# A third quadrant block in each first FFN, and the small parameter operations on GpSimd

## The chip, the cores and the metric

The kernel runs on one core of a Trainium2 chip. TensorE (PE) multiplies, VectorE (DVE) does elementwise work, ScalarE (ACT) copies and applies functions, GpSimd (POOL) does a few small operations and issues the accumulating DMAs, and SyncE's queue (SP) issues the loads. Weights and x lie in HBM; SBUF holds tiles of 128 partitions; matmuls write PSUM banks of 128x512 fp32. The metric is the device time of one execution in microseconds.

## What is computed

Two layers of a streaming encoder on x of 256 x 1024, fp32. Cut to what matters:

```python
x += 0.5 * postnorm(swiglu(prenorm(x)))      # first FFN, D_FF = 2816
x += postnorm(mixer(prenorm(x)))             # S5 scan beside chunk attention
x += 0.5 * postnorm(swiglu(prenorm(x)))      # second FFN

def swiglu(h, w_gate, w_up, w_down):
    return (silu(h @ w_gate) * (h @ w_up)) @ w_down

# S5's parameters, of the layer's inputs alone
dt = exp(log_dt); mag = exp(lr * dt); ang = li * dt
ab_re, ab_im = mag * cos(ang), mag * sin(ang)
den = lr * lr + li * li
f_re = ((ab_re - 1) * lr + ab_im * li) / den
f_im = (ab_im * lr - (ab_re - 1) * li) / den
```

## The kernel before, in words

The 256 rows are two row tiles t of 128. All weights come as 2 x 184 chunks of 128x1024 fp32, in the order of use: 66 of the first FFN, 52 of the mixer, 66 of the second FFN. `load` (line 461) has SP load a chunk into one of 12 `raw` buffers. `halves` (line 467) splits it: ACT copies it to `wh` (rounded, line 371), DVE computes `wl = raw - wh` (line 378), and each product is then three matmuls (line 418): x's high part by `wh` and `wl`, and x's low part by `wh`. For the chunks of `ADDED` (44, 47 and so on to 65 of a first FFN) ACT writes `-wh` into `wl`, and an accumulating DMA on POOL's queue (`add_to`, line 382) adds the chunk.

An FFN has six blocks of columns, five of 512 and one of 256. `ffn` (line 741) does a block in one of two ways. The plain way takes gate and up products for each t. The other, `seven` (line 649), cuts rows, the inner dimension and gate/up into quadrants and takes 7 products of sums of quadrants where the plain way has 8; each product is 12 matmuls of 128x512. The sums of the inputs are made once (`sums`). The weight sums are totals of two chunks each: `total` 1 and 2 on DVE, and totals 3 and 4 (`BY_DMA`) by ACT, which negates a chunk in place, and an accumulating DMA that adds another chunk to it. A quadrant block converts 18 chunks on DVE (14 of products, 4 of the down projection), and evacuates PSUM with DVE and ACT. The down products of a block run inside the block that follows. `SEVEN` (line 31) says which blocks go this way: before, 1 and 3 of each first FFN, and 1 to 4 of each second.

`prep` (line 797) computes S5's parameters for a layer: two exponentials by polynomials on 128x16 values (`exp`), sines and cosines on 128x112 values, the factors `fr` and `fi`, and tables `E` that DVE builds from `ecs` and `esn`. In the kernel before, all its elementwise operations but the memsets are on DVE. POOL's other work is the power of -0.5 of each norm (line 393).

The order is not that of the code. `Graph` records every operation with its engine, an estimated cost and a due time; `schedule` (line 209) places the operations one by one in a list schedule and so fixes the order on each engine; each engine then runs its list in that order. `PREP_AT` and `BIAS_AT` name the chunk whose mark the operations of `prep` and the loads of the attention bias have to follow. A mark of a chunk of a quadrant block stands at that block's start.

Of the kernel before, what the change touches and what calls it, by code (L numbers as in the profile page):

```python
# [17 lines left out]
ALU = mybir.AluOpType  # L18
AX = mybir.AxisListType

P = 128
# [6 lines left out]
SP_LR, SP_LI, SP_DT, SP_D, SP_B = 0, 16, 32, 48, 52  # L28

N_BLK = (512, 512, 512, 512, 512, 256)  # L30
SEVEN = (((1, 3), (1, 2, 3, 4)), ((1, 3), (1, 2, 3, 4)))
FFN_CHUNKS = 66
MIX_CHUNKS = 52
LAYER_CHUNKS = 2 * FFN_CHUNKS + MIX_CHUNKS
# [5 lines left out]
LAG = 3  # L40
TAU = 1.395
MARGIN = {"pre": 10.0, "edge": 4.0, "conv": 7.558, "conv0": 3.423, "task": 7.748, "att0": 37.576, "s50": 37.749, "att1": 28.585, "sums": 3.0, "s51": 29.753, "prep": 40.0}
PREP_AT = (3, 149)
BIAS_AT = 50
LOOK = 0.027
CAP = 5.417
WARM = 16
# [18 lines left out]
class View:  # L66
# [50 lines left out]
    def ap(self):  # L117
        t = self.buf.tile
        for s in self.steps:
            t = s(t)  # L120
        return t
# [202 lines left out]
class Kern:  # L324
# [51 lines left out]
    def tt(self, out, a, b, op):  # L376
        return self.g.op("dve", 0.07 + a.free_size() / 960, [out], [a, b],
                         lambda: self.nc.vector.tensor_tensor(out=out.ap(), in0=a.ap(), in1=b.ap(), op=op))  # L378
# [16 lines left out]
    def stt(self, out, a, s, b, op0=ALU.mult, op1=ALU.add):  # L395
        cost = 0.07 + a.free_size() / 960 + 0.061 * isinstance(s, View)
        return self.g.op("dve", cost, [out], [a, s, b], lambda: self.nc.vector.scalar_tensor_tensor(  # L397
            out=out.ap(), in0=a.ap(), scalar=ap(s), in1=b.ap(), op0=op0, op1=op1))

    def ts(self, out, a, s1, s2=None, op0=ALU.mult, op1=ALU.add):  # L400
        def fn():
            if s2 is None:
                self.nc.vector.tensor_scalar(out=out.ap(), in0=a.ap(), scalar1=ap(s1), scalar2=None, op0=op0)
            else:
                self.nc.vector.tensor_scalar(out=out.ap(), in0=a.ap(), scalar1=ap(s1), scalar2=s2, op0=op0, op1=op1)  # L405
        cost = 0.07 + a.free_size() / 1920 + 0.061 * isinstance(s1, View)
        return self.g.op("dve", cost, [out], [a, s1], fn)
# [333 lines left out]
    def ffn(self, l, f, normed):  # L741
# [5 lines left out]
        for b, wd in enumerate(N_BLK):  # L747
            if b in SEVEN[l][f]:
                if s is None:
# [47 lines left out]
    def prep(self, l):  # L797
        self.mode("prep", "bulk")
        if l == 0:
            self.S = [self.own(f"st{i}", [P, PAIRS, 65], F32) for i in range(2)]  # L800
        after = [self.g.ops[self.mark[(0, PREP_AT[l])]]]
        self.constants(after)
# [5 lines left out]
        self.bias = [[self.blk() for _ in range(2)] for _ in range(2)]  # L808
        early = [self.g.ops[self.mark[(0, l * LAYER_CHUNKS + BIAS_AT)]]]
        for par in range(2):  # L810
            for u in range(2):
                b = self.bias[par][u].rearrange("p (h k) -> p h k", k=256)
# [1 line left out]
                self.memset("pool", b[0:64, :, 192:256], MASK)  # L814
        self.prm = prm
        lr, li = prm[:, SP_LR:SP_LR + 16], prm[:, SP_LI:SP_LI + 16]
        ts, tt, stt = self.ts, self.tt, self.stt

        def tmp(nmx):
            return self.own(f"pt_{nmx}", [P, 16], F32)  # L820

        def exp(o, xin):
            n, r, p = tmp("en"), tmp("er"), tmp("ep")
            ib = self.own("pt_ei", [P, 16], I32)
            ts(n, xin, math.log2(math.e), MAGIC)
            ts(n, n, MAGIC, op0=ALU.subtract)
            stt(r, n, -0.693359375, xin)
            stt(r, n, 2.12194440054690583e-4, r)
            ts(p, r, 1.0 / 5040)
            for k in (720, 120, 24, 6, 2, 1):  # L830
                stt(p, p, 1.0 / k, r, ALU.add, ALU.mult)
            ts(n, n, -127.0, 128.0, ALU.max, ALU.min)
            ts(n, n, 127.0, 8388608.0, ALU.add, ALU.mult)
            self.copy(ib, n)
            stt(o, p, 1.0, ib.bitcast(F32), ALU.add, ALU.mult)

        dt, ld, mag, mag2 = tmp("dt"), tmp("ld"), tmp("mag"), tmp("mag2")
        exp(dt, prm[:, SP_DT:SP_DT + 16])
        tt(ld, lr, dt, ALU.mult)
        exp(mag, ld)  # L840
        tt(mag2, mag, mag, ALU.mult)
        self.mag2 = mag2
        self.act(self.mt[:, :, 1:], mag2.spread(63), AF.Copy)

        wk = [self.blk() for _ in range(2)]
        ang, k, z, sn, cs, m, a = (wk[i // 4][:, (i % 4) * 112:(i % 4) * 112 + 112] for i in range(7))
        angv = ang.rearrange("p (e j) -> p e j", j=16)
        tt(angv[:, 0, :], li, dt, ALU.mult)
        for e in range(1, 7):
            ts(angv[:, e, :], angv[:, 0, :], float(2 ** e))  # L850
        ts(k, ang, 2.0 / math.pi, MAGIC)
# [4 lines left out]
        stt(ang, k, -c1, ang)  # L856
        stt(ang, k, -c2, ang)
        stt(ang, k, -c3, ang)
        tt(z, ang, ang, ALU.mult)
        ts(sn, z, 1.0 / 362880)  # L860
        for q in (-1.0 / 5040, 1.0 / 120, -1.0 / 6):
            stt(sn, sn, q, z, ALU.add, ALU.mult)
# [8 lines left out]
        stt(a, m, -1.0, m, ALU.mult, ALU.max)  # L871
        ts(k, a, -1.0, 1.0)
        ts(a, a, -1.0, 2.0)
        tt(m, m, a, ALU.mult)
        ecs = self.own("ecs", [P, 7, 16], F32)
        esn = self.own("esn", [P, 7, 16], F32)
        ef, sf = ecs.rearrange("p e j -> p (e j)"), esn.rearrange("p e j -> p (e j)")
        tt(ef, cs, k, ALU.mult)
        tt(a, sn, m, ALU.mult)
        tt(ef, ef, a, ALU.subtract)  # L880
        tt(sf, sn, k, ALU.mult)
        tt(a, cs, m, ALU.mult)
        tt(sf, sf, a, ALU.add)
        self.ecs, self.esn = ecs, esn

        ar, ni, nr, den, fr, fi, q = (tmp(s) for s in ("ar", "ni", "nr", "den", "fr", "fi", "q"))
        tt(ar, mag, ecs[:, 0, :], ALU.mult)
        ts(nr, ar, 1.0, op0=ALU.subtract)
        tt(ni, mag, esn[:, 0, :], ALU.mult)
        tt(den, lr, lr, ALU.mult)  # L890
        tt(q, li, li, ALU.mult)
        tt(den, den, q, ALU.add)
        self.recip(den, den)
        tt(fr, nr, lr, ALU.mult)
        tt(q, ni, li, ALU.mult)
        tt(fr, fr, q, ALU.add)
        tt(fr, fr, den, ALU.mult)
        tt(fi, ni, lr, ALU.mult)
        tt(q, nr, li, ALU.mult)
        tt(fi, fi, q, ALU.subtract)  # L900
        tt(fi, fi, den, ALU.mult)

        def half(t, i):
            return t[:, 256 * i:256 * i + 256].rearrange("p (j h) -> p j h", h=16)
# [51 lines left out]
        for e in range(6):  # L956
            k = 2 ** e
# [286 lines left out]
def _one_k(w):  # L1244
    return w.reshape(-1, P, 1024)


def _ffn_chunks(g, u, d, seven):
    gu, dn = [], []
    o = 0  # L1250
    for wd in N_BLK:
        s = slice(o, o + wd)
        if wd == 512:
            gu.append(np.concatenate([_two_k(g[:, s]), _two_k(u[:, s])]))
        else:
            gu.append(_two_k(np.concatenate([g[:, s], u[:, s]], axis=1)))
        dn.append(_one_k(d[s]))
        o += wd
    out = [gu[0]]
    for i in range(1, len(N_BLK)):  # L1260
        if i in seven:
            out += [gu[i][:2], dn[i - 1][:1], gu[i][2:], dn[i - 1][1:]]
        else:
            out += [gu[i], dn[i - 1]]
    out.append(dn[-1])
    return np.concatenate(out)


def _pack(a):
    f = np.float32  # L1270
    wall = []
    for l in range(DEPTH):
        w_in = a["w_in"][l]
        wall.append(_ffn_chunks(a["ffn_w_gate"][l, 0], a["ffn_w_up"][l, 0], a["ffn_w_down"][l, 0], SEVEN[l][0]))
        for blk in (0, 2, 1, 3, 6, 7, 4, 5):
# [51 lines left out]
```

## Time and profile before

| | |
|---|---|
| median of 3 runs (lowest, highest) | 1128.24 us (1126.39, 1130.42) |
| the profiled execution | 1127.01 us |
| its span, first to last instruction | 1125.2 us |
| PE, DVE, ACT, POOL busy | 98%, 85%, 67%, 9% of the span |
| mean granted clock of PE | 0.997 |

Times in the rows count from the start of the span; the 1.8 us between span and execution lie around it. The first FFN of layer 0 takes about the first 190 us, with its block 1 up to about 60, and that of layer 1 begins about 570. An instruction's time in a row is longer than the distance to the next one's start where an engine overlaps the end of one with the start of the next: a DVE operation of 128x1024 shows 1.22 us, and the next starts 1.13 to 1.14 after it.

### The profile page before, as it was taken

How to read it: one execution, taken by the hardware profiler on the slowest of the kernel's cores; microseconds unless marked ns; L12 is line 12 of the kernel's file. 1: busy time of each engine (PE TensorE's matmuls, PEld its weight loads, DVE VectorE, ACT ScalarE, POOL GpSimd, SP SyncE). 2: the span in 40 equal slices, each digit the busy share in tenths (PEclk: the TensorE clock that was granted, in tenths of full speed). 3: DMA queues.
4: the chain of work that ended last, by engine and by line, in shares of the span. 5: the costliest groups of instructions: out<-in, count | busy, mean ns of one | idle time of the engine just before them, and what ended most of it. 6: DMA issues, size and time to landing. Idle time of an engine off the chain costs nothing.

```text
span 1125.2 us, 15956 instructions
## 1 busy us (share of the span) xinstructions
PE 1107.9 (98%) x5728; PEld 885.6 (79%) x5728; DVE 954.2 (85%) x1402; ACT 749.1 (67%) x1066; POOL 99.4 (9%) x131
## 2 busy tenths in 40 slices
PE   8999999999999999999999999999999999999997
PEld 6778788777788888788887888887777888888886
DVE  6998995895977899899899689778959679999983
ACT  6957686647754697577577476856486546878752
POOL 1101111000000031010030011100000002111100
PEclk9999999999999999999999999999999999999999
DMA  9885997545275557899658669964535664789941
GB/s 343 228 314 129 328 295 235 169 136 164 97 251 197 179 122 217 269 283 278 243 162 263 229 181 325 276 213 148 170 112 181 195 212 143 214 219 268 293 167 38
DMA packets 69487, 238.61 MB, mean 212 GB/s; under 512 B 8096, under 2 KB 8864, under 8 KB 69408
## 3 DMA queue, kind: packets, MB, share of 16 engines
q1 hardware_dynamic: 60192, 204.03, 51.2%
q0 software_dynamic: 9216, 33.56, 16.3%
q8 instruction: 45, 0.74, 0.3%
q14 instruction: 34, 0.28, 0.1%
HBM read 202.96 MB, written 1.05 MB: 181 GB/s over the span
## 4 chain that ended last, share of the span: by engine, by line
PE 87%; DVE 5%; issue 2%; ACT 2%; DMA 2%; POOL 1%; SPq 0%; POOLq 0%; DVEq 0%; ACTq 0%
PE ps L418 81%; PE ps L432 4%; DVE wl L378 3%; DMA raw<-in_wall_dram 2%; PE ps L424 1%; DVE blk L378 1%; ACT blk L371 1%; POOL s L393 1%; ACT wh L371 1%; DVE blk L397 1%; DVE raw L378 0%; SPq L354 0%; DVE x L397 0%; DVE s L405 0%; POOLq L1322 0%
## 5 line engine op out<-in xcount | busy, mean ns | idle before, releaser
L418 PE MATMUL ps<-wh,blk 128*128 128x512 f32 x2848 | 878.0, 400 | 4.5 <-DVE blk L378 2.3
L418 PEld LDWEIGHTS ps<-wh,blk 128*128 128x128 f32 x2848 | 530.4, 188 | 127.6 <-DVE blk L378 3.9
L371 ACT ACTIVATE wh<-raw 128x1024 fp32r<-128x1024 f32 (+1 forms) x442 | 456.9, 1053 | 261.0 <-PE ps L418 200.4
L378 DVE TENSOR_TENSOR wl<-raw,wh 128x1024 fp32r<-128x1024 f32 (+1 forms) x426 | 505.7, 1215 | 104.3 <-ACT wh L371 103.7
L418 PE MATMUL ps<-wl,blk 128*128 128x512 f32 x1424 | 524.4, 399 | 0.9 <-DVE wl L378 0.8
L418 PEld LDWEIGHTS ps<-wl,blk 128*128 128x128 f32 x1424 | 267.5, 188 | 63.4 <-DVE wl L378 2.5
L371 ACT ACTIVATE blk<-ps 128x512 fp32r<-128x512 f32 (+4 forms) x156 | 86.5, 561 | 54.8 <-PE ps L432 30.2
L378 DVE TENSOR_TENSOR blk<-ps,blk 128x512 fp32r<-128x512 f32 (+2 forms) x164 | 109.4, 672 | 13.1 <-ACT blk L371 12.7
L432 PE MATMUL ps<-ident,blk 128*128 128x128 f32 x432 | 74.7, 273 | 0.0
L382 POOL DMA_DIRECT2D raw<-raw x48 | 41.6, 867 | 341.3 <-ACT raw L371 261.8
L393 POOL TENSOR_TENSOR s<-s,mhalf 128x1 f32<-128x1 f32 x24 | 32.1, 1338 | 448.3 <-DVE s L405 448.2
L371 ACT ACTIVATE blk<-blk 32x128 f32<-32x128 f32 (+4 forms) x148 | 59.1, 400 | 12.4 <-DVE blk L378 8.6
L432 PEld LDWEIGHTS ps<-ident,blk 128*128 128x128 f32 x432 | 54.6, 140 | 15.9 <-PE ps L418 1.3
L371 ACT ACTIVATE blk<-ps,s 128x512 f32<-128x512 f32 (+1 forms) x68 | 43.7, 655 | 24.6 <-PE ps L418 20.4
L378 DVE TENSOR_TENSOR raw<-raw,raw 128x1024 f32<-128x1024 f32 x48 | 58.1, 1219 | 0.1
L371 ACT ACTIVATE raw<-raw 128x1024 f32<-128x1024 f32 x48 | 50.2, 1053 | 4.3 <-DVE raw L378 3.9
L378 DVE TENSOR_TENSOR blk<-blk,blk 128x512 f32<-128x512 f32 (+3 forms) x70 | 42.3, 627 | 0.0
L371 ACT ACTIVATE blk<-blk,s 128x128 f32<-128x128 f32 (+2 forms) x76 | 34.6, 486 | 6.7 <-DVE blk L378 6.6
L397 DVE SCALAR_TENSOR_TENSOR blk<-blk,s,blk 128x512 f32<-128x512 f32 x44 | 32.0, 746 | 0.9 <-ACT blk L371 0.8
L397 DVE SCALAR_TENSOR_TENSOR blk<-ps,s,blk 128x512 f32<-128x512 f32 (+1 forms) x24 | 15.8, 658 | 9.7 <-ACT blk L371 9.4
L382 POOL DMA_DIRECT2D wl<-raw x16 | 13.8, 865 | 111.7 <-ACT wl L371 56.3
L378 DVE TENSOR_TENSOR blk<-ps,raw 128x512 f32<-128x512 f32 x32 | 19.8, 681 | 4.2 <-PE ps L418 4.2
(100 smaller groups left out, 434.0 us busy)
## 6 DMA issues: line engine op xcount, KB each, us to landing
raw<-in_wall_dram SPq DMA_DIRECT2D x366, 512.0 KB, 5.3
raw<-raw POOLq DMA_DIRECT2D x48, 512.0 KB, 5.3
wl<-raw POOLq DMA_DIRECT2D x16, 512.0 KB, 7.2
gain<-in_gains_dram SPq DMA_DIRECT2D x22, 256.0 KB, 4.3
blk<-in_bias_dram SPq DMA_DIRECT2D x8, 256.0 KB, 4.8
raw<-in_wall_dram SPq DMA_DIRECT2D x4, 256.0 KB, 4.3
blk<-in_sp_dram SPq DMA_DIRECT2D x4, 256.0 KB, 9.3
x<-in_x_dram SPq DMA_DIRECT2D x3, 256.0 KB, 5.8
```

The source lines that it names most:

```text
L371: self.nc.scalar.activation(out=out.ap(), in_=in_.ap(), func=func, **k)
L378: lambda: self.nc.vector.tensor_tensor(out=out.ap(), in0=a.ap(), in1=b.ap(), op=op))
L382: lambda: self.nc.gpsimd.dma_start(out=out.ap(), in_=in_.ap(), accum_op=ALU.add), func="dma")
L393: lambda: self.nc.gpsimd.tensor_tensor(out=out.ap(), in0=a.ap(), in1=b.ap(), op=ALU.pow))
L397: return self.g.op("dve", cost, [out], [a, s, b], lambda: self.nc.vector.scalar_tensor_tensor(out=out.ap(), in0=a.ap(), scalar=ap(s), in1= ...
L418: return self.g.op("pe", cost, [out], [lhsT, rhs], lambda: self.nc.tensor.matmul(out.ap(), lhsT=lhsT.ap(), rhs=rhs.ap(), start=start, stop ...
L424: self.nc.tensor.matmul(out.ap(), lhsT=lhsT.ap(), rhs=rhs.ap(), start=start, stop=stop)
L432: lambda o=o, s=s: self.nc.tensor.transpose(o.ap(), s.ap(), self.ident.ap()))
```

## The change

Block 2 of each first FFN goes the quadrant way too, so blocks 1, 2 and 3 do in a row. In `prep` the helpers `ptt`, `ts` and `stt` put its elementwise operations up to `fr` and `fi` on POOL, at an estimated cost of 0.25 us plus 2.2 ns for an element of a partition; what has a maximum stays on DVE, and so do the casts, the reciprocal, `cmul` and the tables. An `stt` becomes two POOL operations with a tile `pt_mid` between. `prep` may begin at chunk 26 in place of 3 (layer 1: 206 in place of 149), which is the start of block 2; the bias loads follow chunk 62 in place of 50.

```diff
-SEVEN = (((1, 3), (1, 2, 3, 4)), ((1, 3), (1, 2, 3, 4)))
+SEVEN = (((1, 2, 3), (1, 2, 3, 4)), ((1, 2, 3), (1, 2, 3, 4)))
...
-PREP_AT = (3, 149)
-BIAS_AT = 50
+PREP_AT = (26, 206)
+BIAS_AT = 62
...
-        ts, tt, stt = self.ts, self.tt, self.stt
+        tt = self.tt
+        gp = self.nc.gpsimd
+
+        def put(out, ins, fn):
+            self.g.op("pool", 0.25 + out.free_size() * 0.0022, [out], ins, fn)
+
+        def ptt(out, a, b, op):
+            put(out, [a, b], lambda: gp.tensor_tensor(out=out.ap(), in0=a.ap(), in1=b.ap(), op=op))
+
+        def ts(out, a, s1, s2=None, op0=ALU.mult, op1=ALU.add):
+            if op0 == ALU.max:
+                self.ts(out, a, s1, s2, op0, op1)
+            elif s2 is None:
+                put(out, [a], lambda: gp.tensor_scalar(out=out.ap(), in0=a.ap(), scalar1=s1, scalar2=None, op0=op0))
+            else:
+                put(out, [a], lambda: gp.tensor_scalar(out=out.ap(), in0=a.ap(), scalar1=s1, scalar2=s2, op0=op0, op1=op1))
+
+        def stt(out, a, s, b, op0=ALU.mult, op1=ALU.add):
+            if op1 == ALU.max:
+                return self.stt(out, a, s, b, op0, op1)
+            n = out.free_size()
+            mid = self.own(f"pt_mid{n}", [P, n])
+            ts(mid, a, s, op0=op0)
+            ptt(out, mid, b, op1)
...
-        tt(ld, lr, dt, ALU.mult)
+        ptt(ld, lr, dt, ALU.mult)
...
-        tt(ef, cs, k, ALU.mult)
+        ptt(ef, cs, k, ALU.mult)
```

The remaining lines turn `tt` into `ptt` in the same way. What this does to the order on the engines (the numbers in names only tell buffers apart):

POOL in layer 0, before: after the last power of the first norm come the four accumulations of block 1 (totals 3 and 4), then those of block 3.

```order
L393 TENSOR_TENSOR s_69_312<-s_68_308,mhalf_74 128x1
L382 DMA raw_339<-raw_373 128x1024
L382 DMA raw_354<-raw_387 128x1024
L382 DMA raw_304<-raw_254 128x1024
L382 DMA raw_322<-raw_271 128x1024
L382 DMA raw_819<-raw_883 128x1024
L382 DMA raw_857<-raw_906 128x1024
L382 DMA raw_776<-raw_726 128x1024
```

POOL in layer 0, now: `pt_en`, `pt_den`, `pt_q`, `pt_mid` and `pt_er` are tiles of `prep`, `prm` its inputs.

```order
L382 DMA raw_333<-raw_367 128x1024
L382 DMA raw_348<-raw_381 128x1024
L382 DMA raw_298<-raw_248 128x1024
L832 TENSOR_SCALAR pt_en_486<-prm_459 128x16
L824 TENSOR_TENSOR pt_den_493<-prm_459 128x16
L830 TENSOR_SCALAR pt_en_486<-pt_en_486 128x16
L824 TENSOR_TENSOR pt_q_499<-prm_459 128x16
L830 TENSOR_SCALAR pt_mid_443_504<-pt_en_486 128x16
L382 DMA raw_316<-raw_265 128x1024
L824 TENSOR_TENSOR pt_er_518<-pt_mid_443_504,prm_459 128x16
L824 TENSOR_TENSOR pt_den_493<-pt_den_493,pt_q_499 128x16
```

Five operations of `prep` stand between the third and the fourth accumulation of block 1; 18 more and three memsets follow before the accumulations of block 2.

POOL in layer 1, before: the last power of the norm, the four accumulations of block 1, then block 3's first.

```order
L393 TENSOR_TENSOR s_1235_5645<-s_1234_5640,mhalf_74 128x1
L382 DMA raw_5505<-raw_5564 128x1024
L382 DMA raw_5529<-raw_5582 128x1024
L382 DMA raw_5443<-raw_5352 128x1024
L382 DMA raw_5486<-raw_5377 128x1024
L382 DMA raw_6103<-raw_6147 128x1024
```

POOL in layer 1, now, from the first accumulation of block 1 on; the rows left out are nine more operations of `prep`.

```order
L382 DMA raw_5444<-raw_5525 128x1024
L382 DMA raw_5482<-raw_5544 128x1024
L832 TENSOR_SCALAR pt_en_5774<-prm_5746 128x16
...
L830 TENSOR_SCALAR pt_mid_1691_5819<-pt_ep_5813 128x16
L824 TENSOR_TENSOR pt_ep_5813<-pt_mid_1691_5819,pt_er_5797 128x16
L830 TENSOR_SCALAR pt_mid_1692_5830<-pt_ep_5813 128x16
L824 TENSOR_TENSOR pt_ep_5813<-pt_mid_1692_5830,pt_er_5797 128x16
L382 DMA raw_5398<-raw_5313 128x1024
L830 TENSOR_SCALAR pt_mid_1693_5852<-pt_ep_5813 128x16
```

Fourteen operations of `prep` stand between the second and the third accumulation.

DVE in layer 0, now, at the end of block 1: `wl_640 <- raw_316` converts the chunk that the fourth accumulation completes.

```order
L378 TENSOR_TENSOR wl_561<-raw_333,wh_528 128x1024
L378 TENSOR_TENSOR wl_577<-raw_348,wh_557 128x1024
L397 SCALAR_TENSOR_TENSOR blk_592<-blk_189,blk_568 128x512
L378 TENSOR_TENSOR wl_600<-raw_367,wh_489 128x1024
L378 TENSOR_TENSOR wl_613<-raw_381,wh_502 128x1024
L378 TENSOR_TENSOR wl_624<-raw_298,wh_609 128x1024
L397 SCALAR_TENSOR_TENSOR blk_637<-blk_229,blk_537 128x512
L378 TENSOR_TENSOR wl_640<-raw_316,wh_626 128x1024
L378 TENSOR_TENSOR blk_239<-blk_239,blk_189 128x512
L378 TENSOR_TENSOR wl_654<-raw_409,wh_547 128x1024
L397 SCALAR_TENSOR_TENSOR blk_663<-blk_239,blk_659 128x512
L378 TENSOR_TENSOR blk_669<-ps_584,blk_449 128x512
```

From `raw_265 <- raw_381,raw_265`, six rows ahead of the first row here, no operation down to `wl_640` reads PSUM: 9 of 128x1024 and 4 of 128x512. The kernel before has the same pieces there, with one conversion and one addition changed about.

## Rows read from the trace of the kernel before

**Rows 1.** page, part 1: busy time, share of the span, instructions
```profile
PE 1107.9 (98%) x5728; PEld 885.6 (79%) x5728; DVE 954.2 (85%) x1402; ACT 749.1 (67%) x1066; POOL 99.4 (9%) x131
```

**Rows 2.** chain of waits that ended last: start, us, what
```profile
651.79 47.13 PE ps L418 x203
```

**Rows 3.** grouped instructions by shape: busy us, mean ns, idle before
```profile
L378 DVE TENSOR_TENSOR wl<-raw,wh 128x1024 fp32r<-128x1024 f32 x422 | 503.0, 1220 | 101.1 <-ACT wh L371 100.5
L371 ACT ACTIVATE wh<-raw 128x1024 fp32r<-128x1024 f32 x438 | 454.4, 1056 | 257.9 <-PE ps L418 200.4 <-issue 27.7 <-DMA raw<-in_wall_dram 23.4
...
L393 POOL TENSOR_TENSOR s<-s,mhalf 128x1 f32<-128x1 f32 x24 | 32.1, 1338 | 448.3 <-DVE s L405 448.2
...
L397 DVE SCALAR_TENSOR_TENSOR blk<-blk 128x112 f32<-128x112 f32 x16 | 4.3, 268 | 0.1
...
L359 POOL MEMSET raw<- 128x16 f32 x6 | 0.6, 122 | 1.5 <-DVE wl L378 1.5
```

**Rows 4.** windows: length, then busy us (instructions) by engine, clock, DMA
```profile
core 0: us, PE busy (x) PEld busy (x) DVE busy (x) ACT busy (x) POOL busy (x), PEclk, DMA share, GB/s
50.00:75.00 25.00, 24.75 (x107) 19.61 (x106) 24.85 (x44) 14.41 (x15) 0.00 (x0) 1.00 0.97 377
1025.00:1050.00 25.00, 25.00 (x112) 20.18 (x111) 25.00 (x26) 19.90 (x22) 3.22 (x4) 1.00 0.92 253
```

**Rows 5.** timeline of DVE, first FFN, layer 0: start, us, instruction
```profile
41.29 0.69 DVE L378 TENSOR_TENSOR blk<-ps,blk 128x512 fp32r<-128x512 f32 x1
41.89 1.22 DVE L378 TENSOR_TENSOR raw<-raw,raw 128x1024 f32<-128x1024 f32 x1
...
56.86 1.22 DVE L378 TENSOR_TENSOR wl<-raw,wh 128x1024 fp32r<-128x1024 f32 x1
58.00 0.68 DVE L378 TENSOR_TENSOR blk<-ps,blk 128x512 f32<-128x512 f32 x1
```

**Rows 6.** timeline of POOL: three powers
```profile
25.19 0.55 POOL L393 TENSOR_TENSOR s<-s,mhalf 128x1 f32<-128x1 f32 x1 [4.63 <-DVE s L405]
...
396.80 5.47 POOL L393 TENSOR_TENSOR s<-s,mhalf 128x1 f32<-128x1 f32 x1 [6.83 <-DVE s L405]
...
581.15 5.40 POOL L393 TENSOR_TENSOR s<-s,mhalf 128x1 f32<-128x1 f32 x1 [6.89 <-DVE s L405]
```

**Rows 7.** timeline of DVE beside the second of these powers
```profile
396.64 0.68 DVE L378 TENSOR_TENSOR blk<-blk,blk 128x512 f32<-128x512 f32 x1
397.24 2.35 DVE L378 TENSOR_TENSOR wl<-raw,wh 128x1024 fp32r<-128x1024 f32 x2
...
401.79 0.74 DVE L397 SCALAR_TENSOR_TENSOR blk<-ps,s,blk 128x512 f32<-128x512 f32 x1
```

**Rows 8.** timeline of POOL: accumulations in block 1 of both layers
```profile
40.53 0.87 POOL L382 DMA_DIRECT2D raw<-raw  x1 [2.02 <-DVE raw L378]
43.64 0.87 POOL L382 DMA_DIRECT2D raw<-raw  x1 [2.23 <-ACT wh L371]
...
596.32 0.86 POOL L382 DMA_DIRECT2D raw<-raw  x1 [5.49 <-DVE raw L378]
```

**Rows 9.** page, part 6: DMA issues, KB each, us to landing
```profile
raw<-raw POOLq DMA_DIRECT2D x48, 512.0 KB, 5.3
```

**Rows 10.** timeline of PE, end of block 1, layer 0
```profile
59.87 0.74 PE L418 MATMUL ps<-wl,blk 128*128 128x512 f32 x2 [0.24 <-DVE wl L378]
```

**Rows 11.** timeline of DVE, first FFN, layer 1
```profile
599.77 0.68 DVE L378 TENSOR_TENSOR blk<-ps,blk 128x512 fp32r<-128x512 f32 x1
...
611.86 0.68 DVE L378 TENSOR_TENSOR blk<-ps,blk 128x512 f32<-128x512 f32 x1
```

**Rows 12.** windows in the second FFN of layer 0
```profile
460.00:465.00 5.00, 2.54 (x10) 1.61 (x9) 5.00 (x6) 4.14 (x5) 0.00 (x0) 1.00 1.02 399
465.00:470.00 5.00, 4.67 (x13) 3.70 (x14) 4.62 (x9) 1.08 (x2) 0.00 (x0) 0.66 0.77 311
```

**Rows 13.** timeline of DVE, tail of the first FFN of layer 0
```profile
161.64 1.22 DVE L378 TENSOR_TENSOR wl<-raw,wh 128x1024 fp32r<-128x1024 f32 x1
```

More of the change, by code (lines that the diff above doesn't have):

```diff
@@ L838, in prep @@
         exp(dt, prm[:, SP_DT:SP_DT + 16])
-        tt(ld, lr, dt, ALU.mult)
+        ptt(ld, lr, dt, ALU.mult)
         exp(mag, ld)
-        tt(mag2, mag, mag, ALU.mult)
+        ptt(mag2, mag, mag, ALU.mult)
         self.mag2 = mag2
@@ L847, in prep @@
         angv = ang.rearrange("p (e j) -> p e j", j=16)
-        tt(angv[:, 0, :], li, dt, ALU.mult)
+        ptt(angv[:, 0, :], li, dt, ALU.mult)
         for e in range(1, 7):
@@ L858, in prep @@
         stt(ang, k, -c3, ang)
-        tt(z, ang, ang, ALU.mult)
+        ptt(z, ang, ang, ALU.mult)
         ts(sn, z, 1.0 / 362880)
@@ L873, in prep @@
         ts(a, a, -1.0, 2.0)
-        tt(m, m, a, ALU.mult)
+        ptt(m, m, a, ALU.mult)
         ecs = self.own("ecs", [P, 7, 16], F32)
@@ L877, in prep @@
         ef, sf = ecs.rearrange("p e j -> p (e j)"), esn.rearrange("p e j -> p (e j)")
-        tt(ef, cs, k, ALU.mult)
[L879 to L883, printed above, removed]
+        ptt(ef, cs, k, ALU.mult)
+        ptt(a, sn, m, ALU.mult)
+        ptt(ef, ef, a, ALU.subtract)
+        ptt(sf, sn, k, ALU.mult)
+        ptt(a, cs, m, ALU.mult)
+        ptt(sf, sf, a, ALU.add)
         self.ecs, self.esn = ecs, esn
         ar, ni, nr, den, fr, fi, q = (tmp(s) for s in ("ar", "ni", "nr", "den", "fr", "fi", "q"))
-        tt(ar, mag, ecs[:, 0, :], ALU.mult)
+        ptt(ar, mag, ecs[:, 0, :], ALU.mult)
         ts(nr, ar, 1.0, op0=ALU.subtract)
[L889 to L892, printed above, removed]
+        ptt(ni, mag, esn[:, 0, :], ALU.mult)
+        ptt(den, lr, lr, ALU.mult)
+        ptt(q, li, li, ALU.mult)
+        ptt(den, den, q, ALU.add)
         self.recip(den, den)
[L894 to L901, printed above, removed]
+        ptt(fr, nr, lr, ALU.mult)
+        ptt(q, ni, li, ALU.mult)
+        ptt(fr, fr, q, ALU.add)
+        ptt(fr, fr, den, ALU.mult)
+        ptt(fi, ni, lr, ALU.mult)
+        ptt(q, nr, li, ALU.mult)
+        ptt(fi, fi, q, ALU.subtract)
+        ptt(fi, fi, den, ALU.mult)
         def half(t, i):
```

## The prediction

> **What bounds the kernel now.** I read the page's busy shares first. TensorE (PE) is busy for 98% of the span, VectorE (DVE) for 85%, ScalarE (ACT) for 67%, GpSimd (POOL) for 9% [rows 1]. So a matmul taken away is worth its own time as long as nothing new is late. The chain that ended last gives that time: 47.13 us for 203 matmuls in a row, 0.2322 us each [rows 2]. The grouped instructions give prices: one DVE conversion of a chunk shows 1.22 us, one ACT copy of a chunk 1.06, a POOL memset of 128x16 0.12 [rows 3]. Then I read the windows by stage, because the mean of 85% hides what matters here. In 50 to 75 us, in the first FFN of layer 0, DVE is busy for 24.85 of 25 us beside a PE busy for 24.75; in 1025 to 1050, where four quadrant blocks follow each other, DVE is busy for 25.00 and PE too [rows 4]. In these stages DVE is as full as PE, and whatever delays DVE delays PE.
>
> **The change, part by part.**
>
> *Matmuls.* Each layer's block 2 now takes 7 products of 12 matmuls in place of 8. That is 12 a layer, 24 in all: 24 x 0.2322 = **-5.6 us**, if nothing else is late.
>
> *DVE and ACT.* A quadrant block has 18 DVE conversions, 4 DVE totals and 9 narrower operations. In the first FFN, 41.89 to 58.00 holds 11 of the wide and 6 of the narrow [rows 5]; 11 x 1.135 + 6 x 0.605 is 16.1, so those are the prices from start to start. A block is 22 x 1.135 + 9 x 0.605 = 30.4 us of DVE against 132 x 0.2322 = 30.7 of PE. Block 2 adds 10 wide DVE operations a layer (11.4 us), and the small operations that leave for POOL give a good part back (16 of the wider ones held DVE for 4.3 us, 0.27 each as shown [rows 3]). Three such blocks in a row can just run: four in a row do so in 1025 to 1050 with PE full [rows 4]. I take **0**; if this cover fails it is rival 2. ACT gets 10 more copies a layer, 10.6 us, and has a third of its time free: 0.
>
> *SP's queue.* In layer 0 the parameters' load stays among the same weight loads; in layer 1 it moves from the mixer's end to the first FFN, 26 KB among chunks of 512 KB. The larger tables and the bias loads keep their places. I take 0; late accumulations do hold up weight loads behind them, but PE stands by then for the same reason, and it isn't counted twice.
>
> *POOL's queue.* This is the part that decides. Some 108 small operations a layer now run on POOL, in the same queue as the accumulating DMAs that make totals 3 and 4. In the kernel before, POOL's only operations that read SBUF are 24 powers. One takes 0.55 us when DVE is quiet, as at 25.19, but those at 396.80 and 581.15 took 5.47 and 5.40 [rows 6]. What DVE did shows why: from 396.64 it ran a 128x512 operation, two conversions, a total and one more conversion, each with two SBUF inputs; at 401.79 came the first with a PSUM input, and the power ended 0.48 us after that, at 402.27 [rows 7]. So a POOL operation that reads SBUF waits until DVE stops running two-input SBUF operations back to back, and then takes about 0.48. The memsets, which only write, show 0.12 and no such wait [rows 3].
>
> The Trainium skill ("SBUF — State Buffer", section "Who interferes with whom") has a DVE instruction with two SBUF inputs and a GpSimd instruction that reads SBUF contend, with a lock held for one whole instruction by whoever issues first. The trace agrees on who contends, but its wait spans five DVE instructions and not one. By that rule the two engines would alternate; rival 3 prices what it would do here.
>
> *Layer 0.* The third accumulation of block 1 issues at 40.53 and is done at 41.40; the fourth followed at 43.64 [rows 8]. Now five small POOL operations stand between them. The first gets in beside DVE's PSUM operation at 41.29; then, from 41.89 to 58.00, DVE has none with a PSUM input [rows 5], and in the changed order none before the conversion that needs the fourth accumulation (wl_640 <- raw_316). Ahead of it stand 9 wide and 4 narrow operations: 41.89 + 9 x 1.135 + 4 x 0.605 = 54.5. DVE stops there, waiting for a DMA that POOL has not issued, and only that lets POOL in: 4 x 0.48 = 1.9, then 5.3 until an accumulation lands [rows 9], then one ACT copy, 1.1 with the hand-over: **+8.3 us**. PE has no slack: at 59.87 it already waits for a conversion [rows 10]. Ends: 0, if POOL gets in at once; 15, if the operations take 0.7 and the landing doubles.
>
> *Layer 1.* The second accumulation of block 1 issues at 596.32 and is done at 597.18 [rows 8]. Now 14 small operations stand between it and the third. DVE offers one opening, the PSUM operation at 599.77 of 0.68 us, then nothing until 611.86 [rows 11]; I let 2 of the 14 through. DVE reaches the conversion of the third after 6 wide and 2 narrow operations: 599.77 + 6 x 1.135 + 2 x 0.605 = 607.8. Then 12 x 0.48 = 5.8, 5.3 to land, 1.1 for ACT: 12.2, less some 0.9 us by which PE uses the next conversion later: **+11.3 us**. Ends: 0 and 16. The 7 operations ahead of the fourth accumulation run while DVE stands.
>
> *Clock.* In the second FFN of layer 0 PE was busy for 2.54 of 5 us, and in the next 5 the granted clock was 0.66 on average, so between its two levels of 1.2 and 2.4 GHz [rows 12]: 5 x 0.34 = 1.7 us lost. Two longer stalls: **+3.4 us**; ends 0 and 7.
>
> *The rest of prep*, from about 120 us of layer 0 and the same place of layer 1: 85 small POOL operations and 8 DMA issues. DVE's E tables need their end, and behind those stands the conversion that started at 161.64 [rows 13]. No row has a POOL operation of 128x112; by 128x16 memsets below (0.12) and the free power above (0.55) the 85 take 10 to 47 us, near the upper end since they compute; with 7 for the DMAs POOL ends at 137 to 174. That straddles 162: I take 2 a layer, **+4 us**; ends 0 and 20 a layer.
>
> Sum against the profiled execution of 1127.0 us: 1127.0 - 5.6 + 8.3 + 11.3 + 3.4 + 4 = **1148.4 us**. The median of the runs shown is 1.2 us above that execution, which I leave out. A measurement of this kernel tells about 0.3%, 3.4 us, from no change. The stalls may fall short by half (1136) or reach their upper ends (1162); this case's own range is 1132 to 1162.
>
> **The rivals.**
> 1. *POOL gets in.* The small operations with one input, or of 16 elements, may slip between DVE's instructions, so that no accumulation is late. Against it speak the two powers of one element a partition that did not [rows 6]; for it, that only powers show it. Decided by whether the fourth accumulation issues before about 48 us (54.5 less 5.3 and 1.1). Then only the matmuls count: 1121.4, faster. Chance 0.17.
> 2. *DVE's last reserve goes, POOL being harmless.* Three blocks in a row use it up as at 460 to 465, 2.5 us of PE and 1.7 of clock [rows 12], once a layer: 1121.4 + 8.4 = 1129.8, no difference. Chance 0.08.
> 3. *The engines alternate.* Each POOL operation waits for one DVE instruction and then holds DVE for 0.48: a pair takes about 1.45. In layer 0 the accumulation issues in time, but DVE loses 9 x 0.48 = 4.3 by 54.5. In layer 1 some 10 operations pass by 612, 4 are left, and DVE resumes at 620.4, 12.6 late less 0.9: 11.7. Sum: 1127.0 - 5.6 + 4.3 + 11.7 + 3.4 + 4 = 1144.8. The powers' waits speak against it. Chance 0.10. It is what the skill's rule ("SBUF — State Buffer", "Who interferes with whom") would give.
> 4. *The rest of prep starves.* With 10 us a layer, half its upper end, in place of 2: 1164. Speaks for it that the first FFN's tail still needs DVE; against it, that its blocks 4 and 5 evacuate PSUM more often. Chance 0.10.
>
> **How the numbers follow.** The forecast has 0.55. Slower by over 0.3%: 0.55 + 0.10 + 0.10 = 0.75; faster 0.17; same 0.08. The range has to reach rival 1, since the forecast and rivals 3 and 4 alone hold 0.75: 1121 to 1162. It leaves out the worst of rival 4 and a little below rival 1.
>
> **What would show it.** Right: in 41 to 56 us POOL has small operations of 5 to 13 us, ending where DVE idles; the fourth accumulation of block 1 issues after 55 in layer 0 and the third after 611 in layer 1; DVE then idles 7 to 12 us before a conversion, with the DMA as releaser, PE idles as long, and the granted clock falls behind it. Wrong: POOL's small operations take about 0.5 us beside a full DVE, PE's idle time stays as it was, and the span falls by 5 us; or PE's idle time lies elsewhere, after 120 us of a layer, before conversions that stand behind the E tables.

## The result and the profile after

The changed kernel takes 1155.92 us (median of 4 runs, 1155.42 to 1156.6), beside 1127.32 for the kernel before (4 runs now, where 3 stood above). The ratio is 1.0251, with a 95% interval of 1.0238 to 1.0265: slower by 28.6 us. The forecast was 1148.4, in a range of 1121 to 1162. The profiled execution took 1155.64 us, its span 1153.8, 28.6 over the span of before.

The busy shares, to be read beside [rows 1]:

```profile
PE 1113.1 (96%) x5704; PEld 887.4 (77%) x5704; DVE 964.2 (84%) x1276; ACT 769.3 (67%) x1088; POOL 217.7 (19%) x355
```

POOL's busy time has more than doubled, DVE's has risen by 10 us and PE's by 5, with 24 matmuls fewer: PE does no more work, it waits longer and runs part of the time at a lower granted clock. PE's listed waits sum to 33.2 us where they were 10.3. PE's timeline (start, us, instruction, in brackets the idle time before it and what ended that) has these, none of which was there before:

```profile
65.44 0.80 PE L418 MATMUL ps<-wl,blk 128*128 128x512 f32 x1 [7.37 <-DVE wl L378]
...
103.45 0.50 PE L418 MATMUL ps<-wh,blk 128*128 128x512 f32 x1 [1.44 <-DVE blk L378]
...
192.86 1.55 PE L432 MATMUL ps<-ident,blk 128*128 128x128 f32 x6 [5.01 <-ACT blk L371]
...
627.89 1.43 PE L418 MATMUL ps<-wh,blk 128*128 128x512 f32 x5 [0.94 <-DVE blk L397]
...
635.43 0.46 PE L418 MATMUL ps<-wh,blk 128*128 128x512 f32 x1 [2.65 <-ACT wh L371]
...
668.97 0.51 PE L418 MATMUL ps<-wh,blk 128*128 128x512 f32 x1 [1.55 <-DVE blk L378]
...
756.20 0.98 PE L432 MATMUL ps<-ident,blk 128*128 128x128 f32 x4 [4.17 <-ACT blk L371]
```

Four things stand here: block 1 of layer 0 (65.44) and of layer 1 (627.89, 635.43), the end of block 2 (103.45, 668.97), and the transposes of prep's tables (192.86, 756.20). Four more waits of 0.5 to 1.7 us lie at 144 to 188 and at 715. The pair of waits before [rows 12] is gone.

**Block 1 of layer 0.** POOL's timeline:

```profile
41.82 0.88 POOL L382 DMA_DIRECT2D raw<-raw  x1 [2.03 <-DVE raw L378]
42.77 0.20 POOL L832 TENSOR_SCALAR pt_en<-prm 128x16 f32<-128x16 f32 x1
43.05 0.21 POOL L824 TENSOR_TENSOR pt_den<-prm 128x16 f32<-128x16 f32 x1
43.35 12.66 POOL L830 TENSOR_SCALAR pt_en<-pt_en 128x16 f32<-128x16 f32 x1
...
56.28 0.26 POOL L830 TENSOR_SCALAR pt_mid<-pt_en 128x16 f32<-128x16 f32 x1
56.59 0.92 POOL L382 DMA_DIRECT2D raw<-raw  x1
```

One operation of 16 elements a partition took 12.66 us. The fourth accumulation, which issued at 43.64 before [rows 8], issues at 56.59. DVE in that time:

```profile
42.57 0.69 DVE L378 TENSOR_TENSOR blk<-ps,blk 128x512 fp32r<-128x512 f32 x1
...
55.19 0.70 DVE L397 SCALAR_TENSOR_TENSOR blk<-blk,blk 128x512 fp32r<-128x512 f32 x1
62.39 1.24 DVE L378 TENSOR_TENSOR wl<-raw,wh 128x1024 fp32r<-128x1024 f32 x1 [6.50 <-ACT wh L371]
```

The last PSUM operation is the one at 42.57, as in [rows 5]. Then come thirteen instructions with two SBUF inputs, the last until 55.89, and POOL's operation ends at 56.01, 0.12 us after it. DVE then stands for 6.50 us.

**Block 1 of layer 1.** The same operations on POOL:

```profile
606.80 0.86 POOL L382 DMA_DIRECT2D raw<-raw  x1 [2.56 <-ACT raw L371]
...
608.77 1.11 POOL L830 TENSOR_SCALAR pt_en<-pt_en 128x16 f32<-128x16 f32 x1
609.87 1.11 POOL L824 TENSOR_TENSOR pt_q<-prm 128x16 f32<-128x16 f32 x1
...
619.64 0.91 POOL L382 DMA_DIRECT2D raw<-raw  x1
...
625.91 0.89 POOL L382 DMA_DIRECT2D raw<-raw  x1 [0.33 <-issue]
```

Here the operation that took 12.66 us took 1.11, and so did the next. DVE beside them:

```profile
608.53 2.37 DVE L378 TENSOR_TENSOR wl<-raw,wh 128x1024 fp32r<-128x1024 f32 x2
610.82 0.69 DVE L378 TENSOR_TENSOR blk<-blk,blk 128x512 f32<-128x512 f32 x1
...
625.98 1.23 DVE L378 TENSOR_TENSOR wl<-raw,wh 128x1024 fp32r<-128x1024 f32 x1 [1.15 <-ACT wh L371]
```

Operations on POOL now come through at each boundary between DVE's instructions: 609.87 + 1.11 is 610.98, 0.16 after DVE's start at 610.82. They hold DVE up hardly at all: the two conversions from 608.53 take 2.29 us to the next start, 1.145 each where 1.135 was the price. DVE then waits 1.15 us for the third accumulation. The fourth issues at 625.91 and lands late as well, as ACT's timeline shows:

```profile
632.37 2.95 ACT L371 ACTIVATE wh<-raw 128x1024 fp32r<-128x1024 f32 x3 [3.26 <-DMA raw<-raw]
```

**The rest of prep** in layer 0, beginning and end of its chain on POOL:

```profile
133.35 0.19 POOL L832 TENSOR_SCALAR pt_en<-pt_en 128x16 f32<-128x16 f32 x1 [10.62 <-DVE pt_en L405]
...
180.87 1.19 POOL L824 TENSOR_TENSOR pt_fi<-pt_fi,pt_den 128x16 f32<-128x16 f32 x1
```

POOL stood idle for 10.62 us because an operation with a maximum, which stays on DVE (`pt_en`, line 405), ran there only at 133.09, behind conversions that kept DVE busy; the chain then took from 133 to 182. The transposes of its tables stand in PE's order where the planner expected them, and PE waits there.

**The clock.** Windows in which the granted clock was below 1.0 while PE was busy throughout:

```profile
core 0: us, PE busy (x) PEld busy (x) DVE busy (x) ACT busy (x) POOL busy (x), PEclk, DMA share, GB/s
23.00:28.00 5.00, 5.00 (x17) 3.92 (x16) 4.57 (x8) 4.60 (x8) 0.56 (x1) 0.66 1.03 408
65.44:72.00 6.56, 6.56 (x17) 5.18 (x18) 6.56 (x8) 1.48 (x2) 0.00 (x0) 0.56 0.87 314
192.86:198.00 5.14, 5.14 (x22) 4.32 (x22) 4.24 (x9) 4.61 (x13) 0.00 (x0) 0.54 0.67 214
757.00:762.00 5.00, 5.00 (x22) 3.98 (x22) 3.49 (x10) 3.86 (x11) 0.00 (x0) 0.66 0.55 106
```

Behind each of the waits of 7.37, 5.01 and 4.17 us the granted clock was 0.54 to 0.66 on average, between its two levels, 1.2 and 2.4 GHz. The loss is the length times what is missing: 2.9, 2.4 and 1.7 us, and 1.7 in the first window. Before, only the window after [rows 12] lost 1.7. So 7.0 us net.

Added up: listed waits 33.2 - 10.3 = 22.9, clock 7.0, matmuls -5.6, together 24.3 of 28.6 us. Of the other 4.3 us, 3.8 lie in PE's busy time, which rose by 5.2 where clock and matmuls make 1.4; what they are stays open.

### The profile page after: what moved, and what is told of

Same layout as the page of the kernel before. It is cut to its first block, busy times and chain, and to the rows that moved or that the text cites. A ratio compares the mean times of both kernels' runs of the same rounds, so it can differ in the third digit from the quotient of the medians.

```text
span 1153.8 us, 16025 instructions
## 1 busy us (share of the span) xinstructions
PE 1113.1 (96%) x5704; PEld 887.4 (77%) x5704; DVE 964.2 (84%) x1276; ACT 769.3 (67%) x1088; POOL 217.7 (19%) x355
## 4 chain that ended last, share of the span: by engine, by line
PE 69%; DVE 10%; POOL 10%; issue 4%; DMA 4%; ACT 3%; SPq 0%; POOLq 0%; DVEq 0%; ACTq 0%
PE ps L418 64%; DVE wl L378 4%; PE ps L432 4%; DVE blk L378 3%; DMA raw<-in_wall_dram 3%; POOL pt_mid L830 2%; DVE raw L378 2%; ACT blk L371 1%; PE ps L424 1%; POOL pt_en L830 1%; POOL blk L824 1%; ACT wh L371 1%; POOL blk L830 1%; DMA raw<-raw 1%; DVE blk L397 1%
## 5 line engine op out<-in xcount | busy, mean ns | idle before, releaser
L371 ACT ACTIVATE wh<-raw 128x1024 fp32r<-128x1024 f32 (+1 forms) x454 | 468.2, 1052 | 256.6 <-PE ps L418 187.4
L378 DVE TENSOR_TENSOR wl<-raw,wh 128x1024 fp32r<-128x1024 f32 (+1 forms) x438 | 520.0, 1219 | 89.2 <-ACT wh L371 88.7
L378 DVE TENSOR_TENSOR blk<-ps,blk 128x512 f32<-128x512 f32 (+2 forms) x174 | 117.0, 676 | 17.5 <-ACT blk L371 12.2
L382 POOL DMA_DIRECT2D raw<-raw x56 | 48.8, 871 | 296.6 <-ACT raw L371 163.2
L378 DVE TENSOR_TENSOR raw<-raw,raw 128x1024 f32<-128x1024 f32 x56 | 68.0, 1225 | 0.0
L371 ACT ACTIVATE raw<-raw 128x1024 f32<-128x1024 f32 x56 | 58.7, 1054 | 6.1 <-DVE raw L378 5.0
L378 DVE TENSOR_TENSOR blk<-blk,blk 128x512 f32<-128x512 f32 (+1 forms) x68 | 41.9, 640 | 0.0
L397 DVE SCALAR_TENSOR_TENSOR blk<-blk,s,blk 128x512 f32<-128x512 f32 x48 | 35.2, 750 | 0.7 <-POOL s L393 0.6
L359 POOL MEMSET blk<- 128x512 f32 (+1 forms) x26 | 12.3, 507 | 80.5 <-PE ps L432 32.2
L397 DVE SCALAR_TENSOR_TENSOR blk<-ps,s,blk 128x512 f32<-128x512 f32 (+1 forms) x20 | 12.8, 642 | 13.4 <-ACT blk L371 12.2
```

The source lines that it names most:

```text
L359: lambda: getattr(self.nc, name).memset(out.ap(), v), after=after)
L371: self.nc.scalar.activation(out=out.ap(), in_=in_.ap(), func=func, **k)
L382: lambda: self.nc.gpsimd.dma_start(out=out.ap(), in_=in_.ap(), accum_op=ALU.add), func="dma")
```

## The experiments

All twelve are given as edits of the changed kernel, unless said. The median of the kernel before was 1126.7 to 1128.3 in their comparisons.

**prep_dve: prep back on DVE.**

```diff
...
-        def put(out, ins, fn):
...
+        ts, tt, stt = self.ts, self.tt, self.stt
+        ptt = tt
```

> The changed kernel with the operations of prep back on DVE (start at chunk 26 and bias loads at 62 kept). Theory, that POOL's small operations make the loss: PE's idle 7.4 us at 58 to 65 and 5.0 at 188 to 193 of layer 0, and those of layer 1, go; 1121 to 1130 us. Rival, that three quadrant blocks in a row are more than DVE can carry: still over 1140, since DVE now has some 9 us a layer more, and PE waits for conversions in blocks 2 and 3.

Measured: 1127.17 us, ratio 1.0001 (0.9989 to 1.0013). The stalls of block 1 and the 5.0 and 4.2 us at prep's end are gone, as the theory said. So having these operations on POOL costs 28.7 us, and block 2 in quadrants, with 24 matmuls less, brings nothing. That is the second part to explain. PE waits 1.79 us at the end of block 2 and ACT, before it, for a load (PE's and ACT's timelines):

```profile
94.43 0.50 PE L418 MATMUL ps<-wh,blk 128*128 128x512 f32 x1 [1.79 <-DVE blk L378]
```

```profile
87.44 2.01 ACT L371 ACTIVATE wh<-raw 128x1024 fp32r<-128x1024 f32 x2 [5.92 <-DMA raw<-in_wall_dram]
```

**seven_only: the kernel before, with block 2 in quadrants alone.**

```diff
-SEVEN = (((1, 3), (1, 2, 3, 4)), ((1, 3), (1, 2, 3, 4)))
+SEVEN = (((1, 2, 3), (1, 2, 3, 4)), ((1, 2, 3), (1, 2, 3, 4)))
```

> The kernel before with block 2 in quadrants and nothing else (prep on DVE from chunk 3). Theory: 24 matmuls less and DVE holds out: 1121 to 1126 us. Rival, that DVE's reserve goes: 1130 or more, with PE idle for 2 us or more in blocks 2 and 3 of each first FFN.

Measured: 1132.3 us, ratio 1.0041 (1.0028 to 1.0054). The rival's time, though its mechanism is not shown by it: PE waits 1.67 and 1.72 us at the end of block 2, and 1.70 and 3.15 at prep's end. It is 5.1 us slower than prep_dve, from which it differs only by the earlier start of `prep` and of the bias loads; so these two settings matter as well.

**memsets: the same places in POOL's queue, nothing read.**

```diff
-            self.g.op("pool", 0.25 + out.free_size() * 0.0022, [out], ins, fn)
+            self.g.op("pool", 0.25 + out.free_size() * 0.0022, [out], ins, lambda: gp.memset(out.ap(), 1.0))
```

> The changed kernel, each of prep's 108 POOL operations a layer replaced by a POOL memset of the same tile at the same place of POOL's queue (S5's parameters are then constants); every engine's order is that of the changed kernel. Theory, that reading SBUF beside DVE is what delays POOL: memsets take 0.12 to 0.2 us, no POOL operation takes over 2 us, the fourth accumulation of block 1 issues before 46 us, and the time falls to 1121 to 1130. Rival, that the place in POOL's queue and the number of operations is enough: the accumulations are still late and the time is 1145 or more.

Measured: 1128.59 us, ratio 1.0017 (1.0004 to 1.0029), within what was expected. POOL's timeline has five memsets between the third and the fourth accumulation, POOL then waits 1.85 us for ACT, and the fourth issues at 42.90:

```profile
39.80 0.87 POOL L382 DMA_DIRECT2D raw<-raw  x1 [2.04 <-DVE raw L378]
40.34 0.45 POOL L821 MEMSET pt_en<- 128x16 f32 x1
...
42.90 0.87 POOL L382 DMA_DIRECT2D raw<-raw  x1 [1.85 <-ACT wh L371]
```

So a place in the queue and the number of instructions are not enough, it is what the operations do: 27.3 of the 28.7 us go with it. Memsets are also shorter, 0.11 us against 0.2 to 0.26 of an undisturbed operation of 16 elements. Five such lengths are about 1 us, too little for the 13 us of block 1; there it is the shut-out, which no memset shows. At prep's end, with 85 of them, this run doesn't separate reading from length, but the timeline of the changed kernel helps: in layer 0 the 85 took 43.3 us, and by the usual undisturbed lengths there (0.25 and 0.22 us for 16 elements, 0.49 and 0.42 for 112, for one and two inputs) they would take some 29, an estimate. So most of prep's time on POOL is the operations' own length, and about a third is waiting.

**after_adds: no operation among block 1's accumulations.**

```diff
...
+        late = after + [self.adds[7 * l]]
...
-        self.dma(prm, self.sp_d[l, :, 0:SP_B], after)
+        self.dma(prm, self.sp_d[l, :, 0:SP_B], late)
```

> The changed kernel with prep's parameters loaded only after the fourth accumulation of block 1 in each layer, so that no small operation stands among block 1's accumulations. Theory: the stalls before the conversions of block 1 go (7.4 us of PE and some 2 of clock in layer 0, 3.6 in layer 1), those at the end of prep stay: about 1143 us, 1139 to 1147. Rival, that the delay is only handed on (prep ends later by as much, or block 2's accumulations are late in place of block 1's): 1150 or more.

Measured: 1158.65 us, ratio 1.0277 (1.0262 to 1.0292). The rival was right. The stalls of block 1 are gone, but the operations now stand among the accumulations of block 2, and one is shut out in layer 1 for 12.49 us:

```profile
67.26 0.92 POOL L382 DMA_DIRECT2D raw<-raw  x1
...
79.43 0.91 POOL L382 DMA_DIRECT2D raw<-raw  x1
...
640.00 12.49 POOL L826 TENSOR_TENSOR pt_er<-pt_mid,pt_er 128x16 f32<-128x16 f32 x1
```

PE waits 4.07 us at 98 and 5.74 at 661.

**first_pool and rest_pool: one part of prep on POOL each.** The first keeps the operations of the first exponential there (22 a layer), the second 83 of the others (the three that make `den` go to DVE too).

```diff
         exp(dt, prm[:, SP_DT:SP_DT + 16])
+        ts, ptt, stt = self.ts, self.tt, self.stt
```

```diff
+        pool = ts, ptt, stt
+        ts, ptt, stt = self.ts, self.tt, self.stt
         exp(dt, prm[:, SP_DT:SP_DT + 16])
+        ts, ptt, stt = pool
...
```

> The changed kernel with only the first exponential of prep (its 23 operations of 128x16 in each layer) on POOL, the rest back on DVE. Theory, that the loss adds up from two places: block 1's stalls stay (7.4 us of PE and some 3 of clock in layer 0; in layer 1 up to 4 when the operations take turns with DVE, up to 12 when one is shut out), the stall of 4 to 5 us at the end of prep goes: 1138 to 1146 us. Rival, that the end of prep is what costs and block 1's delay is caught up: under 1133.

> The changed kernel with the first exponential back on DVE and the other 85 POOL operations a layer kept. Theory: no operation stands among block 1's accumulations, so PE's stall of 7.4 us at 58 to 65 goes; the stalls at the end of prep (5.0 and 4.2 us of PE, 1 to 2 us each for late conversions, some 5 of clock) stay: 1138 to 1146 us. Rival, that the late end comes from the late first exponential: under 1133.

Measured: 1137.43 us, ratio 1.0096 (1.0078 to 1.0113), and 1150.88, ratio 1.0209 (1.0195 to 1.0223). Against prep_dve they cost 10.3 and 23.7 us, together 34.0, where both cost 28.7, so the parts don't simply add. Alone, the 83 operations at the end cost more than twice what the first exponential does, on which the forecast put most. The expectation of 1138 to 1146 was too low for them, and a little too high for the first exponential. In first_pool an operation is shut out at 41.9 for 12.60 us.

**prep_only: prep on POOL, block 2 plain.**

```diff
-SEVEN = (((1, 2, 3), (1, 2, 3, 4)), ((1, 2, 3), (1, 2, 3, 4)))
+SEVEN = (((1, 3), (1, 2, 3, 4)), ((1, 3), (1, 2, 3, 4)))
...
-        after = [self.g.ops[self.mark[(0, PREP_AT[l])]]]
+        after = [self.g.ops[self.first[20 + l * LAYER_CHUNKS]]]
```

> Prep on POOL as in the changed kernel, starting with the load of chunk 20, but block 2 plain as before. Theory: five operations again stand between the third and the fourth accumulation of block 1, so its stall is there (about 8 us of PE in layer 0), while the plain blocks let prep end in time: 1134 to 1146 us. Rival, that POOL's operations only hurt when DVE is full through block 2 as well: 1124 to 1130.

Measured: 1150.16 us, ratio 1.0208 (1.0187 to 1.0229), above both expectations. Prep on POOL alone costs some 23 us without the third quadrant block. The shut-out is there, and now the accumulations into `wl` are late too (POOL's, then PE's timeline):

```profile
41.78 14.41 POOL L831 TENSOR_SCALAR pt_en<-pt_en 128x16 f32<-128x16 f32 x1
```

```profile
150.18 0.72 PE L418 MATMUL ps<-wl,blk 128*128 128x512 f32 x1 [4.46 <-DMA wl<-raw]
```

**relief: prep_dve, with two chunks of block 2 made by ACT and an accumulating DMA.**

```diff
-ADDED = range(44, 66, 3)
+ADDED = (29, 30, *range(44, 66, 3))
```

> Prep on DVE, block 2 in quadrants, and two of block 2's down chunks (29 and 30 of each layer) made by ACT and an accumulating DMA, so that DVE has 2.3 us less to do in block 2. Theory, that the 5.6 us of the matmuls were given back to a full DVE: PE's waits of 1.8 and 1.3 us at the end of block 2 go, 1122 to 1125 us. Rival, that the accumulating DMA is late instead or other waits take their place: 1127 or more.

Measured: 1138.85 us, ratio 1.011 (1.0094 to 1.0127). The theory fell: with less work for DVE the kernel is 11.7 us slower than prep_dve. ACT waits for loads:

```profile
91.69 1.06 ACT L371 ACTIVATE wh<-raw 128x1024 fp32r<-128x1024 f32 x1 [3.29 <-DMA raw<-in_wall_dram]
```

PE waits 1.58 us at 95, where it waited 1.79, and then 1.96 for `wh`. The edit adds work for ACT and the DMA queue too, so by itself it doesn't clear DVE. The window of prep_dve from 80 to 90 us, shown in the next experiment, does: DVE stands there for 2.3 of the 10 us, while ACT waits for a load.

**raw14: prep_dve, with 14 buffers for raw chunks.**

```diff
-SLOTS = {"blk": 33, "ps": 8, "wh": 8, "wl": 8, "raw": 12, "gain": 2,
+SLOTS = {"blk": 33, "ps": 8, "wh": 7, "wl": 7, "raw": 14, "gain": 2,
```

> Prep on DVE and block 2 in quadrants, with 14 raw buffers in place of 12 (7 wh and 7 wl in place of 8 each). Theory, that the 5.6 us of the 24 matmuls were given back because the loads of blocks 2 and 3 come late for want of raw buffers, which the totals hold longer: ACT's wait for a load of 5.9 us at 82 to 87 shrinks, PE's stalls of 1.8 and 1.3 us at the end of block 2 go, 1122 to 1125 us. Rival, that the DMA engines (busy share 1.0 from 80 to 95 us) or DVE set the pace: stalls as they were, 1126 to 1130.

Measured: 1127.36 us, ratio 0.9999 (0.9988 to 1.001). Half of the theory holds. Windows of raw14, then of prep_dve, at the end of block 2:

```profile
80.00:90.00 10.00, 10.00 (x45) 8.08 (x44) 10.00 (x10) 6.64 (x8) 0.00 (x0) 1.00 1.02 308
90.00:95.00 5.00, 5.00 (x24) 4.02 (x23) 5.00 (x6) 2.65 (x4) 0.00 (x0) 1.00 1.03 414
```

```profile
80.00:90.00 10.00, 10.00 (x45) 7.97 (x44) 7.74 (x8) 3.77 (x5) 0.00 (x0) 1.00 1.01 286
90.00:95.00 5.00, 3.21 (x15) 2.30 (x15) 5.00 (x6) 4.62 (x5) 0.00 (x0) 1.00 1.02 414
```

PE no longer waits there (1.79 us before) although the DMA engines are as full, so it was the buffers that held the loads back. But the time did not fall: PE's listed waits fell only from 15.4 to 15.1 us, with 2.04 and 1.76 at prep's end.

**pad: one memset ahead of the operation that was shut out.**

```diff
-            ts(n, n, MAGIC, op0=ALU.subtract)
+            pad = self.own("pt_pad", [P, 16], F32)
+            self.g.op("pool", 0.285, [n, pad], [n], lambda: (
+                gp.memset(pad.ap(), 0.0),
+                gp.tensor_scalar(out=n.ap(), in0=n.ap(), scalar1=MAGIC, scalar2=None, op0=ALU.subtract)))
```

> The changed kernel with one POOL memset of 128x16 ahead of the second operation of each exponential, the one that took 12.66 us in layer 0 and 1.11 in layer 1; all other order is kept, so that operation comes to DVE about 0.08 us later. Theory, that it is chance, a matter of the moment at which it asks, whether a POOL operation takes turns with DVE or is shut out: it takes about 1.1 us now, the fourth accumulation issues before 49 us, PE's stall of 7.4 us at 58 to 65 falls below 2, and the time to 1145 to 1150. Rival, that the stretch of DVE's instructions decides: 12 us again, 1154 to 1158.

Measured: 1155.96 us, ratio 1.0242 (1.022 to 1.0264). The rival was right; this shift of about 0.1 us changes nothing:

```profile
43.53 0.11 POOL L851 MEMSET pt_pad<- 128x16 f32 x1
43.72 12.60 POOL L852 TENSOR_SCALAR pt_en<-pt_en 128x16 f32<-128x16 f32 x1
...
609.00 0.10 POOL L851 MEMSET pt_pad<- 128x16 f32 x1
609.19 1.07 POOL L852 TENSOR_SCALAR pt_en<-pt_en 128x16 f32<-128x16 f32 x1
```

**priced: a price of 0.9 us in the planner.**

```diff
-            self.g.op("pool", 0.25 + out.free_size() * 0.0022, [out], ins, fn)
+            self.g.op("pool", 0.9, [out], ins, fn)
...
-MARGIN = {... "prep": 40.0}
+MARGIN = {... "prep": 45.0}
```

> The changed kernel with the planner's price of a small POOL operation at 0.9 us, near what they took in block 1 of layer 1, and prep's margin at 45 in place of 40; two operations stand ahead of the fourth accumulation of layer 0 in place of five, and prep's parts are planned further apart. Theory: the order can't be repaired by a price, since one operation that is shut out is enough and the end of prep stays late: 1140 to 1156. Rival, that the estimated cost alone was wrong: 1122 to 1132.

Measured: 1181.1 us, ratio 1.0472 (1.0454 to 1.0491), worse than either expectation. The fourth accumulation is in time, the operation after it is shut out for 13.60 us, block 2's are late by 6.64 us of PE, and prep's end costs PE 9.30 and 6.55 us in layer 0 and 9.28 and 7.44 in layer 1.

**raw14_m60: raw14, with prep's margin at 60.**

```diff
-MARGIN = {... "prep": 40.0}
+MARGIN = {... "prep": 60.0}
```

> The kernel with prep on DVE, block 2 in quadrants and 14 raw buffers, with the planner's margin for prep at 60 in place of 40, so that prep's last operations are planned earlier. Theory, that what is left of the 5.6 us is given back where PE waits for prep's tables (2.0 us at 173 in layer 0, 1.8 at 727 in layer 1): these go, and the time is 1122 to 1125. Rival, that DVE then has the same operations ahead of conversions, which come late in their place: 1126 to 1130.

Measured: 1160.24 us, ratio 1.029 (1.0273 to 1.0307); the theory fell by far, and so did the rival. An earlier due time moves PE's transposes forward too, ahead of what DVE and ACT deliver:

```profile
163.15 1.97 PE L432 MATMUL ps<-ident,blk 128*128 128x128 f32 x8 [5.89 <-ACT blk L371]
168.00 0.79 PE L418 MATMUL ps<-wh,blk 128*128 128x512 f32 x1 [2.89 <-ACT blk L371]
```

## Why the prediction was right, and where not

*The direction and most of the size.* The time lies 7.5 us above the forecast, in its range and in that of its own case, 1132 to 1162. What it rested on is shown: without POOL's operations the loss is gone (prep_dve), and with writes alone in the same places too (memsets).

*Layer 0's stall (+8.3).* Measured 7.37 us of PE. DVE was to stop 12.6 us after its last PSUM operation and did (42.57 + 0.60 to 55.89 is 12.7); the accumulation was to issue 1.9 us later and issued after 0.7, because an operation alone takes 0.2 to 0.3 with its hand-over and not 0.48.

*Layer 1's stall (+11.3).* The weak step: measured 3.6. Two things failed. The accumulation at 596.32 was taken for block 1's second, and it is its third (the second issued at 589.96), so the operations had 6.4 us more. And the sentence that a POOL operation waits until DVE stops is no law. Of the 216 small operations in the changed kernel, counted in the timeline, 169 took up to 0.6 us, 46 took 0.6 to 1.7, mostly one DVE instruction's length, and one 12.66. The fourteen took 11.9 us by turns, so DVE's idle time before the conversion of the third, foretold as 7 to 12 us, was 1.15. The rule of the Trainium skill that was weighed ("SBUF — State Buffer", section "Who interferes with whom"), one whole instruction for whoever came first, describes the 46; the 12.66 it does not.

*The clock (+3.4).* Measured 7.0: there were three long waits and not two, and a fourth fall after a short one.

*The rest of prep (+4).* Measured 7.0 us of PE's waits in layer 0 and 5.8 in layer 1. The failed step is the start, not the price: from 133.35 to 182.06 the chain took 49 us with six accumulations among it, near the upper bound of 54, but it began 13 us later than assumed, behind a DVE operation, and of a term whose ends were 0 and 20 us a layer 2 were taken. And it was not the conversions behind the E tables that made most of it, but PE's transposes.

*DVE's cover (0).* Wrong in its consequence: the 5.6 us were given back, as rival 2 had it (1129.8; prep_dve has 1127.2). Its mechanism was wrong, though: raw buffers and late loads at the end of block 2 (raw14), and prep's end, not a full DVE (the window of prep_dve from 80 to 90 us). In raw14, 4.8 of the 5.6 us stand in PE's listed waits (15.1 against 10.3 in the kernel before), 3.8 of them at prep's end; no run here brought these back, so that they are what takes the saving is read from the trace and not shown by an edit.

*Rival 3* had the right mechanism for layer 1, but the hold of 0.48 us on DVE isn't there (1.145 against 1.135 a conversion). *Rival 1* is excluded by 43.35 alone. Layer 1's error of 7.7 us too much and prep's end of 8.8 too little nearly cancel: that the sum was better than its terms is luck.

## What to carry to other kernels

Before a small operation is moved to an idle engine, look at what stands behind it in that engine's queue: here four DMA issues, on which TensorE's next block waited. An engine's mean share says nothing of that: POOL was at 9%, and one operation of 16 elements a partition cost TensorE 7 us. And where the work that is saved ends in a fixed order, the first thing to become late (here buffers for loads and, by TensorE's waits, one chain of small operations) takes the saving back.

## What the runs showed that was not expected

Whether DVE shuts POOL out or takes turns depends on the stretch of DVE's instructions, as far as these kernels show, and not on the POOL operation. The stretch from about 42 to 56 us in layer 0 (to 58 in priced) shut one out in all five kernels that had one there: 12.66, 12.60 (first_pool, another operation), 14.41 (prep_only), 12.60 (pad) and 13.60 us (priced). The same operation beside the same kinds of instructions in layer 1 took 1.11, or 1.07 with the memset ahead of it. It isn't that place alone: after_adds has its 12.49 us in block 2 of layer 1, and priced one of 5.88 at 72 us. Each operation that was shut out ended within 0.2 us of the end of a DVE instruction behind which DVE stood, or of the start of one that reads PSUM. What tells the stretches apart wasn't found.

The wait of 1.8 us before PE's instruction at 22.4 is in the kernel before and in the changed one alike. The window behind it had a granted clock of 1.00 in the one and 0.66 in the other (of before, with the one behind [rows 12]):

```profile
23.00:28.00 5.00, 5.00 (x22) 3.66 (x21) 4.57 (x8) 4.97 (x9) 0.55 (x1) 1.00 1.02 406
465.33:470.00 4.67, 4.67 (x13) 3.70 (x14) 4.29 (x8) 1.08 (x2) 0.00 (x0) 0.63 0.76 304
```
